# An eight-expert two-layer MLP on one core: TensorE's inner loop cut from eight columns to four, and one critical section in place of two

## The chip, the core and the metric

The kernel runs on one NeuronCore of a Trainium2 chip. Its engines run side by side, each with its own instruction stream: TensorE (PE in the profile; its weight loads are the row PEld), VectorE (DVE), ScalarE (ACT), GpSimd (POOL) and SyncE (SP). A letter q behind a name (PEldq, SPq) means the engine's sequencer, which reads the instructions one after the other, carries out the register, branch and semaphore instructions itself and hands the rest on. Sixteen DMA engines move data between HBM and the core's memory SBUF. TensorE writes its results to a second memory, PSUM, which ScalarE and VectorE read.

The metric is the device time of one execution in microseconds (us), the median of several runs.

## The reference

```python
n_experts, capacity, hidden, expert_hidden = 8, 256, 512, 2048
...
h = np.matmul(x, w1) + b1[:, np.newaxis, :]
h = np.maximum(h, 0)
return (np.matmul(h, w2) + b2[:, np.newaxis, :]).astype(np.float32)
```

For each of eight experts, 256 rows of 512 values are multiplied by a 512 x 2048 matrix, a bias is added and negative values are set to zero; the result is multiplied by a 2048 x 512 matrix and a second bias is added. Inputs and outputs are float32 in HBM. The weights are 8 MB per expert, 64 MB in all.

## The kernel before

**Loading.** GpSimd issues the weight loads (`load_w1`, `load_w2`, both through `load`, line 91), in float32 from HBM to float16 in SBUF. Each of w1 and w2 has three buffers (`NW = 3`); the load into a buffer that was used waits until the matmuls of the expert before have read it. SyncE loads the inputs of experts 0 and 1 at the start, and GpSimd the other inputs in two groups. ScalarE loads the first bias.

**Transposing.** VectorE casts the first two inputs to float16 and transposes each expert's input in 32 x 32 blocks (`transposes`, lines 176 and 179).

**TensorE.** Its program is a loop over eleven steps (line 279). Step s does the first matmul of expert s (if s < 8, line 290) and then the second matmul of expert s - 3 (if s >= 3, lines 311 and 314). The first matmul is cut into 16 columns j of 128 hidden units; a column is four matmuls (kc = 0 to 3) that accumulate into one of four PSUM banks (`j % NPH`). An inner loop (line 286) runs over the columns: before the change it has eight columns in its body and goes round twice per expert. The semaphore `s_credit` counts free banks: the first matmul of column j waits for j + 1, ScalarE adds one when it has read a bank, and at the end of the loop body (line 300) TensorE's sequencer takes off as many as the body has columns. The second matmul is 16 + 16 matmuls of 512 columns into two PSUM banks, each with one matmul for the bias ahead (line 311). TensorE waits for weights and inputs by `take` (line 274). [...]

**Reading PSUM.** ScalarE turns each column of the first matmul into float16 with bias and relu (line 227); it also copies one of the two output banks (line 191), VectorE the other. ScalarE's order is: the sixteen columns of expert s, then the copies of expert s - 3.

**Handing weights over.** SyncE waits for each load's semaphore and adds to `s_go` (`go`, line 240), which `take` consumes. The results of experts 0 to 3 and of 4 and 5 are stored by GpSimd in two large stores (`flush`), those of experts 6 and 7 by SyncE (`store`, line 244), whose last one waits for both output copies (line 264).

**Sections.** All of this stands in one critical section (lines 83 to 325), whose start and end are synchronised by ScalarE: every engine waits for ScalarE's signal before it enters. A second section (line 326) has SyncE wait for the four stores. Then the engines meet at a barrier (line 354).

Of the kernel before, what the change touches and what calls it, by code (L numbers as in the profile page):

```python
# [10 lines left out]
def kernel(  # L11
# [12 lines left out]
    nc = tc.nc  # L24
# [3 lines left out]
    PE = mybir.EngineType.PE  # L28
    E, T, H = x.shape
    M = w1.shape[2]  # L30
    P = 128
    nTB = T // P
    nKC = H // P
    nJ = M // P
    half = nJ // 2
    B = 32
    nB = P // B
    LAG = 3
    NW = 3
    NPH = 4  # L40
    GROUPS = {0: 4, 4: 2}
    HALVED = (E - 2, E - 1)
# [7 lines left out]
    def sem(name):  # L50
        return ctx.enter_context(nc.semaphore(name=name))
# [21 lines left out]
    results = {}  # L73
    for first, n in GROUPS.items():
# [4 lines left out]
    ph = ctx.enter_context(nc.psum_tensor("ph", [P, NPH, H], fp32))  # L79
    po = ctx.enter_context(nc.psum_tensor("po", [P, 2 * nTB * H], fp32))  # L80

    section = ctx.enter_context(ExitStack())
    section.enter_context(tc.tile_critical(  # L83
        sync_engine=mybir.EngineType.Activation, no_gpsimd_drain=True))


    landed = {}

    def load(engine, key, **kw):
        landed[key] = sem(f"d_{key}")  # L90
        engine.dma_start(**kw).then_inc(landed[key], 16)  # L91
# [6 lines left out]
    s_credit = sem("ph_free")  # L98
# [24 lines left out]
    def load_w2(e):  # L123
        if e >= NW:
            nc.gpsimd.wait_ge(s_po[1], e - NW + 1)
        dst = w2_sb[:, e % NW * nJ * H : (e % NW + 1) * nJ * H].rearrange("p (j h) -> p j h", j=nJ)
        src = w2[e].rearrange("(p j) h -> p j h", j=nJ)
        size = half if e in HALVED else nJ
        for lo in range(0, nJ, size):
            load(nc.gpsimd, f"w2_{e}_{lo}", out=dst[:, lo : lo + size], in_=src[:, lo : lo + size])  # L130

    def flush(first):
        n = GROUPS[first]
        for tb in range(nTB):
            nc.gpsimd.wait_ge(s_out[tb], first + n)
        load(nc.gpsimd, f"out{first}", in_=results[first][:],
             out=out[first : first + n].rearrange("e (p r) h -> (e p) r h", r=n * nTB))
# [3 lines left out]
         in_=b2.rearrange("e h -> (e h)").rearrange("(o f) -> o f", o=1))  # L141
    for s in range(1, E + LAG - 1):
# [4 lines left out]
        if s >= LAG:  # L147
            load_w2(s - LAG)
    load_w2(E - 1)
    for first in GROUPS:  # L150
        flush(first)


    nc.vector.memset(ones1[:], 1.0).then_inc(s_ones, 1)  # L154
    nc.scalar.wait_ge(s_ones, 1)
    nc.scalar.activation(out=warm[:], in_=ones1[:], func=relu)  # L156
# [48 lines left out]
    for b in range(nB):  # L205
        last = nc.vector.transpose(  # L206
            out=b1T[b * B : (b + 1) * B, nB - 1 - b : nB - 1 - b + nJ * B],
            in_=b1_rows[:].rearrange("r (i j) -> r j i", j=nJ),
# [9 lines left out]
    for s in range(E + LAG):  # L218
        if s < E:
# [3 lines left out]
            for j in range(nJ):  # L223
# [4 lines left out]
                    out=hT[:, at : at + T].rearrange("p (tb k i) -> p tb k i", tb=nTB, k=split),  # L228
                    in_=ph[:, j % NPH, 0:T].rearrange("p (tb i k) -> p tb k i", tb=nTB, k=split),
# [11 lines left out]

    def store(e, p0, p1, engine):
        dst = out[e].rearrange("(p r) h -> p r h", r=nTB)
        load(engine, f"out{e}_{p0}", out=dst[p0:p1], in_=results[e][p0:p1])

    for s in range(E + LAG):
        if s == 0:
            nc.sync.wait_ge(landed["b2"], 16)
        if s < E:
            go(f"w1_{s}")  # L250
        e = s - LAG
        if e >= 0 and e not in HALVED:
            go(f"w2_{e}_0", 2)
        elif e == E - 2:
            go(f"w2_{e}_0")
            go(f"w2_{e}_{half}")
        elif e == E - 1:
            go(f"w2_{e}_0")
            for tb in range(nTB):
                nc.sync.wait_ge(s_out[tb], e)  # L260
            store(E - 2, 0, P, nc.sync)
            go(f"w2_{e}_{half}")
    for tb in range(nTB):
        nc.sync.wait_ge(s_out[tb], E)
    store(E - 1, 0, P, nc.sync)


    nc.tensor.sem_inc(s_credit, NPH)
# [4 lines left out]
    def take(s, n=1):  # L273
        nc.tensor.wait_ge(s, n).then_inc(s, -n)  # L274

    def at(value, most):
        return nc.tensor.snap(value.with_bounds(min_val=0, max_val=most))

    with nc.Fori(0, E + LAG, 1, engines=[PE], head_slot={PE: 0}) as s:
        nc.tensor.wait_ge(s_credit, NPH)  # L280
        w_at = at(s % NW * (nKC * M), (NW - 1) * nKC * M)
        with nc.tensor.If(s < E):
            x_at = at((s & 1) * (nKC * T), nKC * T)
            take(s_go)
            take(s_xT)
            with nc.Fori(w_at, w_at + nJ, half, engines=[PE]) as w_from:
                w_from = w_from.with_bounds(min_val=0, max_val=(NW - 1) * nKC * M + half)
                for j in range(half):
                    for kc in range(nKC):
                        last = nc.tensor.matmul(  # L290
                            ph[:, j % NPH, 0:T],
                            w1_sb[:, bass.ds(w_from + (kc * M + j), P, nJ)],
                            xT[:, bass.ds(x_at + kc * T, T)],
                            start=(kc == 0),
                            stop=(kc == nKC - 1),
                        )
                        if kc == 0:
                            last.wait_op(s_credit, j + 1, "sem-ge")
                    last.then_inc(s_ph, 1)
                nc.tensor.sem_inc(s_credit, -half)  # L300
        with nc.tensor.If(s >= LAG):
            b_at = at((s - LAG) * H, (E - 1) * H)
            h_at = at(((s + 1) & LAG) * (nJ * T), LAG * nJ * T)
            p_at = at(((s + 1) & 1) * (nTB * H), nTB * H)
            for lo in range(0, nJ, half):
                take(s_go)
                for tb in range(nTB):
                    bank = po[:, bass.ds(p_at + tb * H, H)]
                    if lo == 0:
                        take(s_free[tb])  # L310
                        nc.tensor.matmul(bank, ones1[:], b2_sb[:, bass.ds(b_at, H)],  # L311
                                         start=True, stop=False)
                    for j in range(lo, lo + half):
                        last = nc.tensor.matmul(  # L314
                            bank,
                            hT[:, bass.ds(h_at + (j * T + tb * P), P)],
                            w2_sb[:, bass.ds(w_at + j * H, H)],
                            start=False,
                            stop=(j == nJ - 1),
                        )  # L320
                    if lo:
                        last.then_inc(s_po[tb], 1)


    section.close()
    with tc.tile_critical(sync_engine=mybir.EngineType.SP, no_gpsimd_drain=True):
        for key in (*(f"out{first}" for first in GROUPS), f"out{E - 2}_0", f"out{E - 1}_0"):
            nc.sync.wait_ge(landed[key], 16)


# [28 lines left out]
```

## Time and profile before

| quantity | value |
|---|---|
| median of 3 runs | 183.68 us (182.99 to 183.78) |
| the profiled execution's own time | 183.61 us |
| its span, first to last instruction | 181.8 us |
| mean granted TensorE clock | 0.967 |
| PE busy | 136.5 us (75%) |
| DVE / ACT busy | 87.5 us (48%) / 72.8 us (40%) |
| bytes read from and written to HBM | 71.39 MB and 4.19 MB, 416 GB/s over the span |

The profiled execution's time is 1.8 us more than its span, and 0.07 us under the median of the runs. Times in rows are from the start of the span. In a row of a timeline stand the start, the duration, the engine and line, the operation, its tiles, how many instructions are merged, and in brackets the idle time of that engine before it and what ended it. A row of a list of one line's instructions gives their count, the shortest, median and longest duration in ns, and the first and last start. A row of a table by stretches gives the busy time of each engine, the granted clock, the mean busy share of the 16 DMA engines, and GB/s. In the strips over 40 slices each digit is a busy share in tenths.

### The profile page before, as it was taken

What the parts mean: (1) busy time and instruction counts of PE and PEld (TensorE: products, weight loads), DVE (VectorE), ACT (ScalarE), POOL (GpSimd) and SP (SyncE); (2) the same over time, 40 slices, a digit from 0 to 9 for tenths busy, and PEclk for the clock granted to TensorE, in tenths of its full rate; (3) what the DMA queues carried; (4) which work ended last, traced back from release to release, by engine and by line L of the source; (5) the groups of instructions that cost most, each with busy time, mean ns of one, the idle gap of its engine ahead of it and who ended that gap; (6) DMA issues with size and microseconds to landing.
All of it is one profiled execution on the core that took longest, in us unless ns stands there. A gap on an engine that the chain in (4) does not pass through costs nothing. (4 is left out here: it accounts for less than half of the span.)

```text
span 181.8 us, 3006 instructions
## 1 busy us (share of the span) xinstructions
PE 136.5 (75%) x784; PEld 92.8 (51%) x784; DVE 87.5 (48%) x125; ACT 72.8 (40%) x152; POOL 12.5 (7%) x27
## 2 busy tenths in 40 slices
PE   0000996969969794897988797879799797999940
PEld 0000894859858541694468544874389333444310
DVE  0999936739000199998199708990600030301010
ACT  3000494767747505383077505770397102011010
POOL 6000003020020101001010001000200003010000
PEclk9999997899997999699999999999999999999997
DMA  5989998999999999999999999999999999999991
GB/s 190 282 187 222 231 223 187 223 231 222 196 220 205 241 198 220 227 220 198 220 231 216 198 220 231 220 195 220 231 223 195 216 209 218 213 218 227 419 407 53
DMA packets 3827, 40.48 MB, mean 223 GB/s; under 512 B 448, under 2 KB 464, under 8 KB 1136
## 3 DMA queue, kind: packets, MB, share of 16 engines
q0 software_dynamic: 3200, 38.28, 95.2%
q1 hardware_dynamic: 576, 2.10, 3.1%
q10 hardware_dynamic: 48, 0.07, 0.1%
q8 instruction: 1, 0.02, 0.0%
q14 instruction: 2, 0.02, 0.0%
HBM read 71.39 MB, written 4.19 MB: 416 GB/s over the span
## 5 line engine op out<-in xcount | busy, mean ns | idle before, releaser
L290 PE MATMUL ph<-xT,w_sb 128*128 x512 | 73.6, 309 | 31.9 <-PEq L274 29.8
L290 PEld LDWEIGHTS ph<-xT,w_sb 128*128 x512 | 67.2, 147 | 39.3 <-issue 32.3
L227 ACT ACTIVATE hT<-ph,b1T 128x256 f16<-128x256 f32 x128 | 58.5, 474 | 37.5 <-PE ph L290 34.8
L179 DVE STREAM_TRANSPOSE xT<-x 32x256 f16<-32x256 f16 (+1 forms) x64 | 52.8, 895 | 26.6 <-DMA x<-in_x_dram 21.8
L314 PE MATMUL po<-w_sb,hT 128*128 x256 | 58.2, 380 | 0.3
L314 PEld LDWEIGHTS po<-w_sb,hT 128*128 x256 | 24.2, 98 | 30.5 <-issue 4.8
L191 DVE COPY out<-po 32x512 f32<-32x512 f32 (+1 forms) x20 | 13.7, 687 | 40.9 <-PE po L314 40.6
L191 ACT COPY out<-po 32x512 f32<-32x512 f32 (+1 forms) x20 | 11.6, 578 | 49.9 <-PE po L314 49.8
L91 POOL DMA_DIRECT2D w_sb<-in_w_dram x18 | 9.8, 545 | 139.4 <-PE po L314 72.3
L176 DVE STREAM_TRANSPOSE xT<-x 32x256 f16<-32x256 f16 x32 | 13.9, 436 | 0.5
L311 PE MATMUL po<-b_sb,ones 1*128 x16 | 6.1, 379 | 5.9 <-PEq L274 5.9
L191 DVE COPY x<-po 128x512 f32<-128x512 f32 x2 | 1.4, 692 | 13.7 <-PE po L314 13.7
L311 PEld LDWEIGHTS po<-b_sb,ones 1*128 1x128 f16 x16 | 1.4, 90 | 11.4 <-issue 11.4
L191 ACT COPY x<-po 128x512 f32<-128x512 f32 x2 | 1.2, 585 | 14.0 <-PE po L314 14.0
L206 DVE STREAM_TRANSPOSE b1T<-b_rows 32x512 f32<-32x512 f32 x4 | 4.1, 1022 | 0.1
L200 DVE CAST x<-x 128x1024 f16<-128x1024 f32 x2 | 1.4, 694 | 3.3 <-DMA x<-in_x_dram 3.3
L91 POOL DMA_DIRECT2D out_dram<-out x2 | 1.1, 540 | 9.0 <-ACT out L191 9.0
L156 ACT ACT_TABLE_LOAD x1 | 1.3, 1283 | 1.0 <-ACTq L83 1.0
L91 POOL DMA_DIRECT2D x<-in_x_dram x2 | 1.1, 557 | 0.0
L154 DVE MEMSET ones<- 1x128 f16 x1 | 0.2, 165 | 1.0 <-ACTq L83 1.0
L91 POOL DMA_DIRECT2D b_sb<-in_b_dram x1 | 0.5, 507 | 0.0
L156 ACT ACTIVATE warm<-ones 1x128 f16<-1x128 f16 x1 | 0.3, 308 | 0.0
(4 smaller groups left out, 0.4 us busy)
## 6 DMA issues: line engine op xcount, KB each, us to landing
w_sb<-in_w_dram POOLq DMA_DIRECT2D x14, 2048.0 KB, 40.1
w_sb<-in_w_dram POOLq DMA_DIRECT2D x4, 1024.0 KB, 22.2
out_dram<-out POOLq DMA_DIRECT2D x1, 2048.0 KB, 25.5
x<-in_x_dram SPq DMA_DIRECT2D x2, 512.0 KB, 5.9
x<-in_x_dram POOLq DMA_DIRECT2D x1, 1024.0 KB, 33.9
out_dram<-out POOLq DMA_DIRECT2D x1, 1024.0 KB, 18.7
out_dram<-x SPq DMA_DIRECT2D x2, 512.0 KB, 7.4
x<-in_x_dram POOLq DMA_DIRECT2D x1, 512.0 KB, 25.8
```

The lines of the kernel that those rows point to most:

```text
L91: engine.dma_start(**kw).then_inc(landed[key], 16)
L154: nc.vector.memset(ones1[:], 1.0).then_inc(s_ones, 1)
L156: nc.scalar.activation(out=warm[:], in_=ones1[:], func=relu)
L176: last = nc.vector.transpose(out=dst[:, :, g, :, 0, :], in_=block[:, :, :, 0, :])
L179: last = nc.vector.transpose(out=dst[:, tb, g], in_=block[:, tb])
L191: last = copy(out=results[e][at : at + rows, k * nTB + tb, :], in_=po[k * rows : (k + 1) * rows, bank : bank + H])
L200: nc.vector.tensor_copy(out=x16[e][0][:], in_=x32[e][:]).then_inc(s_self, 1)
L206: last = nc.vector.transpose(out=b1T[b * B : (b + 1) * B, nB - 1 - b : nB - 1 - b + nJ * B], in_=b1_rows[:].rearrange("r (i j) -> r j i", ...
L227: nc.scalar.activation(out=hT[:, at : at + T].rearrange("p (tb k i) -> p tb k i", tb=nTB, k=split), in_=ph[:, j % NPH, 0:T].rearrange("p ( ...
L290: last = nc.tensor.matmul(ph[:, j % NPH, 0:T], w1_sb[:, bass.ds(w_from + (kc * M + j), P, nJ)], xT[:, bass.ds(x_at + kc * T, T)], start=(k ...
L311: nc.tensor.matmul(bank, ones1[:], b2_sb[:, bass.ds(b_at, H)], start=True, stop=False)
L314: last = nc.tensor.matmul(bank, hT[:, bass.ds(h_at + (j * T + tb * P), P)], w2_sb[:, bass.ds(w_at + j * H, H)], start=False, stop=(j == nJ ...
```

## The change

There are three parts.

1. The inner loop of the first matmul has four columns (`NPH`) in its body and goes round four times per expert. Bank `j % NPH` becomes bank `j`; the sequencer takes off four credits at the end of each body. TensorE's instruction listing has 121 rows after the change, 155 before. [...]
2. One section instead of two. It is synchronised by SyncE. The two large stores are awaited by SyncE inside the section, at its end; the last two stores count on a semaphore of their own, `s_last`, which is awaited behind the section. VectorE adds 32 to it ahead of the section and takes 32 off inside it.
3. A call ahead of GpSimd's two stores (`wait_critical_data_deps`) takes GpSimd's wait for the section's start out of the entry and puts it there: GpSimd enters without waiting, and issues the weight loads at once.

```diff
+    s_last = sem("last_stores")
+    nc.vector.sem_inc(s_last, 16 * len(HALVED))
...
-        sync_engine=mybir.EngineType.Activation, no_gpsimd_drain=True))
+        sync_engine=mybir.EngineType.SP, no_gpsimd_drain=True))
...
     load_w2(E - 1)
+    tc.wait_critical_data_deps()
     for first in GROUPS:
         flush(first)
...
+    nc.vector.sem_inc(s_last, -16 * len(HALVED))
     nc.vector.memset(ones1[:], 1.0).then_inc(s_ones, 1)
...
-        load(engine, f"out{e}_{p0}", out=dst[p0:p1], in_=results[e][p0:p1])
+        engine.dma_start(out=dst[p0:p1], in_=results[e][p0:p1]).then_inc(s_last, 16)
...
     store(E - 1, 0, P, nc.sync)
+    for first in GROUPS:
+        nc.sync.wait_ge(landed[f"out{first}"], 16)
...
-    with nc.Fori(0, E + LAG, 1, engines=[PE], head_slot={PE: 0}) as s:
+    with nc.Fori(0, E + LAG, 1, engines=[PE]) as s:
...
-            with nc.Fori(w_at, w_at + nJ, half, engines=[PE]) as w_from:
-                w_from = w_from.with_bounds(min_val=0, max_val=(NW - 1) * nKC * M + half)
-                for j in range(half):
+            with nc.Fori(w_at, w_at + nJ, NPH, engines=[PE]) as w_from:
+                w_from = w_from.with_bounds(min_val=0, max_val=(NW - 1) * nKC * M + nJ - NPH)
+                for j in range(NPH):
...
-                            ph[:, j % NPH, 0:T],
+                            ph[:, j, 0:T],
...
-                nc.tensor.sem_inc(s_credit, -half)
+                nc.tensor.sem_inc(s_credit, -NPH)
...
     section.close()
-    with tc.tile_critical(sync_engine=mybir.EngineType.SP, no_gpsimd_drain=True):
-        for key in (*(f"out{first}" for first in GROUPS), f"out{E - 2}_0", f"out{E - 1}_0"):
-            nc.sync.wait_ge(landed[key], 16)
+    nc.sync.wait_ge(s_last, 16 * len(HALVED))
```

## The prediction

> **What bounds the kernel now.** I read the strips of the page first, then the waits of TensorE and SyncE, then TensorE's timeline.
>
> ```profile
> DMA  5989998999999999999999999999999999999991
> q8 instruction: 1, 0.02, 0.0%
> ...
> PE ph L290 <- PEq L274: 29.8, 8, 17.9
> ...
> SPq L240 <- DMA w_sb<-in_w_dram: 150.2, 17, 14.6
> ```
>
> The DMA engines are busy from end to end, and SyncE spends 150.2 us waiting for weights. But how far is TensorE behind them? The next fence puts TensorE's starts beside the moments at which SyncE hands over w1 of experts 4, 5 and 6 (line 240).
>
> ```profile
> 17.87 9.82 PE L290 MATMUL ph<-xT,w_sb 128*128 x64 [17.87 <-PEq L274]
> 29.47 9.68 PE L290 MATMUL ph<-xT,w_sb 128*128 x64 [1.78 <-PEq L274]
> 40.93 4.38 PE L290 MATMUL ph<-xT,w_sb 128*128 x32 [1.78 <-PEq L274]
> 52.02 9.30 PE L290 MATMUL ph<-xT,w_sb 128*128 x64 [1.77 <-PEq L274]
> 62.30 0.37 PE L311 MATMUL po<-b_sb,ones 1*128 x1 [0.98 <-PEq L274]
> 64.83 5.35 PE L314 MATMUL po<-w_sb,hT 128*128 x24
> 73.54 9.57 PE L290 MATMUL ph<-xT,w_sb 128*128 x64 [3.35 <-PEq L274]
> ...
> L240 SPq EVENT_SEMAPHORE  x1: 17/17/17, 72.6 to 72.6; - x1
> L240 SPq EVENT_SEMAPHORE  x1: 17/17/17, 92.0 to 92.0; - x1
> L240 SPq EVENT_SEMAPHORE  x1: 17/17/17, 111.4 to 111.4; - x1
> ...
> 105.71 5.35 PE L314 MATMUL po<-w_sb,hT 128*128 x24
> 112.24 4.38 PE L290 MATMUL ph<-xT,w_sb 128*128 x32 [1.18 <-PEq L274]
> 117.15 4.39 PE L290 MATMUL ph<-xT,w_sb 128*128 x32 [0.53 <-ACT hT L227]
> 122.51 0.37 PE L311 MATMUL po<-b_sb,ones 1*128 x1 [0.96 <-PEq L274]
> ...
> w_sb<-in_w_dram POOLq DMA_DIRECT2D x14, 2048.0 KB, 40.1
> ```
>
> Weights come every 19.4 us (72.6, 92.0, 111.4). TensorE ends a step at 105.71 + 5.35 = 111.06, only 0.3 us before the weights of the next. Once, ahead of expert 4, it has slack: done at 64.83 + 5.35 = 70.18, weights at 72.6, 2.4 us. So DMA and TensorE are nearly level: what makes a step of TensorE longer by more than about 0.3 us makes TensorE the bound. The weight loads are issued 40.1 us ahead of their landing, four loads deep, so a TensorE that is some us late in freeing a buffer does not let the DMA engines run dry.
>
> **Part 1, the inner loop.** What does one closing of the loop cost? TensorE's sequencer, near 116 us:
>
> ```profile
> L300 PEldq EVENT_SEMAPHORE  x1: 51/51/51, 116.3 to 116.3; - x1
> L286 PEldq FUSED_REGOPS  x1: 42/42/42, 116.5 to 116.5; - x1
> L286 PEldq COMPARE_BRANCH  x1: 215/215/215, 116.6 to 116.6; - x1
> L290 PEldq FUSED_REGOPS  x4: 46/60/79, 116.1 to 117.2; - x4
> ...
> 117.14 0.60 PEld L290 LDWEIGHTS ph<-xT,w_sb 128*128 x4 [0.72 <-ACT hT L227]
> ...
> 111.10 2.34 ACT L191 COPY out<-po 32x512 f32<-32x512 f32 x4 [8.38 <-PE po L314]
> 113.63 3.50 ACT L227 ACTIVATE hT<-ph,b1T 128x256 f16<-128x256 f32 x8 [0.19 <-PE ph L290]
> 117.98 0.47 ACT L227 ACTIVATE hT<-ph,b1T 128x256 f16<-128x256 f32 x1 [0.85 <-PE ph L290]
> ```
>
> The profile puts the 0.72 us of idle weight loads at 117.14 down to ScalarE. But ScalarE had read all eight columns by 113.63 + 3.50 = 117.13 and then waited itself for TensorE; the ninth column needs only the bank of the fifth. The idle time is filled by the sequencer: 0.7 us from the semaphore at 116.3 past the branch to the first register operation. Inside the body the loads follow without a gap. After the branch the first four register operations take up to 79 ns in place of 46, about 0.1 us more. I take 0.84 us a closing. Per expert the loop closes after columns 4, 8 and 12 in place of 8: two more, 1.7 us of sequencer time. The bounds: nothing, if the wait really is ScalarE's (ScalarE reads a column in 0.47 us whatever the loop); 0.9 us a closing, if it also starts slower.
>
> Steps 0 to 3 wait for no weights but the first. Their starts lie 11.60, 11.46, 11.09 and 10.28 us apart (17.87, 29.47, 40.93, 52.02, 62.30). The third ran at full clock and shows the sequencer's pace; with 1.7 us more it takes 12.8, and the first two, slowed by the clock at their start, come to the same pace. The fourth takes 12.0. Sum 50.4 in place of 44.4: 6.0 us more, beyond the 2.4 us of slack. From expert 4 on TensorE waits for nothing.
>
> A step of TensorE that waits for nothing: from the end of the second matmul (111.06) ScalarE copies until 113.44 and frees the first bank at 113.63 + 0.47 = 114.1, 3.0 us after; the fifth column needs it, and the closing after column 4 is hidden there. From 114.1 to the next bias matmul (122.51) are 8.4 us with one closing, 9.2 with two. From the bias matmul to the end of the second matmul are 70.18 - 62.30 = 7.9. Sum 3.0 + 9.2 + 7.9 = 20.1, against 19.4 between weights. Four such steps, 80.4 us.
>
> At the end, experts 5 to 7, and the close:
>
> ```profile
> 150.91 0.37 PE L311 MATMUL po<-b_sb,ones 1*128 x1 [1.17 <-PEq L274]
> 168.95 5.64 PE L314 MATMUL po<-w_sb,hT 128*128 x24
> L91 SPq DMA_DIRECT2D out_dram<-x x1: 344/344/344, 175.3 to 175.3; - x1
> DMA to landing us min/median/max: 5.1/5.1/5.1
> ...
> 178.00:179.00 1.00, 0.00 (x0) 0.00 (x0) 0.00 (x0) 0.00 (x0) 0.00 (x0) 1.00 0.06 25
> 179.00:180.00 1.00, 0.00 (x0) 0.00 (x0) 0.00 (x0) 0.00 (x0) 0.00 (x0) 1.00 0.06 25
> ...
> L354 SPq EVENT_SEMAPHORE  x5: 28/28/4345, 176.1 to 181.0; - x5
> ```
>
> They take 168.95 + 5.64 - 150.91 = 23.7 us, and the last store is issued 0.7 us after (175.3 against 174.59). It lands in 5.1 us, of which the last 2.0 (178 to 180) have a DMA share of 0.06, one engine of sixteen: one engine is late, and everything that counts sixteen landings is as late. With idle DMA engines I take 3.0 us for the landing (bounds 2.6 and 5.1).
>
> **Part 1, the instruction block.** What makes one engine late? In the window 4 to 7 us the DMA view has an instruction transfer:
>
> ```profile
> q8 instruction: 1, 0.02, 2.0%
> ```
>
> 2.0% of 16 engines over 3 us is 0.96 us on one engine, on the way of the first weights. It is the only transfer of its queue, 16 KB. If it is TensorE's next block, a program within one block does without, and the first weights land about 1.0 us earlier (bounds 0 and the 2.0 us of the end). No row names the engine it serves; two chances in three that it goes.
>
> [...]
>
> **Parts 2 and 3.** GpSimd's first load starts at 1.48, after a wait for ScalarE until 1.04. Its own barrier ends at 0.6.
>
> ```profile
> 1.48 0.67 POOL L91 DMA_DIRECT2D w_sb<-in_w_dram  x1 [1.04 <-ACTq L83]
> L343 POOLq EVENT_SEMAPHORE  x2: 17/17/17, 0.5 to 0.6; - x2
> ```
>
> So its loads can move up by at most 0.4 us (1.04 - 0.6); SyncE's loads of the inputs go to the same DMA engines at that time, so I take 0.1 (bounds 0 and 0.4). GpSimd's wait for the section's start, now ahead of its two large stores, has long been met there. SyncE gives the section's signal itself, and the other engines enter when they did. VectorE's two semaphore instructions cost nothing beside its wait for the input. Behind the last landing SyncE has, from 180.4 (176.1 + 4.3) on, three more waits, a branch and the second section's signals until 181.2; now one signal and the barrier remain. I take 0.5 us off (bounds 0.7, and 0.3 more should GpSimd, which now leaves the section later, be late at the barrier). The waits for the two large stores end earlier than the last store does; behind them on SyncE stands only the close.
>
> **The sum.** First matmul 17.87 - 1.0 - 0.1 = 16.8; + 50.4 + 7.9 + 80.4 + 23.7 = 179.2, end of TensorE's work; + 0.7 to the store, + 3.0 landing = 182.9; + 0.9 (181.8 - 180.4 - 0.5) = 183.8, the span; + 1.8 outside it: 185.6, against 183.61 for the execution read and 183.68 for the median.
>
> **Rivals.**
>
> 1. *The closings are hidden* (the wait was ScalarE's, or the sequencer runs ahead), and the block's transfer is gone. Then DMA stays the bound, all sixteen engines end together: 183.61 - 2.0 - 0.5 = 181.1. For it speaks the releaser that the profile names; against it ScalarE's 0.85 us of waiting at 117.98. It decides if a closing costs under about 0.3 us. [...] The branch's row has 215 ns, and it is one of several instructions.
> 2. *The block's transfer stays*, the closings cost: 186.6.
> 3. *The block's transfer stays and the closings are hidden*: the change does only its part 2: 183.0.
> 4. *The clock.* TensorE's first matmul gets thinner, and the clock is halved for a stretch after a thin one:
>
> ```profile
> 50.29:53.70 3.41, 1.68 (x13) 1.66 (x13) 0.00 (x0) 1.26 (x3) 1.06 (x2) 1.00 0.90 192
> 53.70:57.12 3.42, 3.42 (x19) 2.70 (x18) 0.00 (x0) 2.04 (x5) 0.00 (x0) 0.50 0.99 208
> 60.53:63.94 3.41, 2.41 (x14) 1.36 (x13) 1.01 (x1) 1.23 (x3) 0.53 (x1) 1.00 1.13 240
> ```
>
> Busy 1.68 of 3.41 us was followed by half clock, 2.41 was not. A stretch with one end of the first matmul and a closing or two comes between. Half clock over 3.4 us of the second matmul costs 1.7: 187.3 with one such stretch, more with two.
>
> **How the numbers follow.** The forecast case 0.44 (its own range 184.4 to 186.8: 0.1 us on a closing's price is 0.2 us in each of the steps 0 to 3 and 0.1 in each of the next four, 1.2 in all); rival 1 0.18, rival 2 0.18, rival 3 0.08, rival 4 0.12. The range goes from rival 1 to rival 4: 181.0 to 188.2. About 0.5% (0.9 us) is what a measurement can tell from no change. Slower by more: the forecast case almost whole, rivals 2 and 4, 0.68; faster: rival 1, 0.19; the rest 0.13.
>
> **What would show it.** Right: starts of line 290 (299 in the changed file) 12.8 us apart; idle weight loads of 0.7 us after every fourth column; no q8 row; no TensorE wait for weights after expert 3; bias matmuls 20.1 us apart from expert 0 to 4; DMA share falling well before the last store. Wrong: bias matmuls still 19.4 us apart with waits at `take`, or a q8 row as before.

## The result and the profile after

The changed kernel takes 184.23 us (median; 184.13 to 184.60), the kernel before 183.26 us beside it: a ratio of 1.0055 (95% interval 1.0040 to 1.0071), 1.0 us slower. The forecast was 185.6, on the right side and inside its range, but 1.4 us high. The kernel before came out lower as well, 183.26 in place of the 183.68 that the prediction had. So the forecast loss was 1.9 us and the measured one 1.0.

The profiled execution has a span of 182.7 us and a time of 184.60. Its strips of DMA and clock, and the last rows of its DMA queues:

```profile
DMA  5989998999999998999999999999899989999972
...
PEclk9999998898899999999999999999999999999999
...
q10 hardware_dynamic: 48, 0.07, 0.1%
q14 instruction: 2, 0.02, 0.0%
```

The q8 row, which stood between these two in the kernel before, is gone, and the DMA strip falls to 7 and 2 before the end, where it stood at 9 to the last slice but one. TensorE's timeline (start, duration, engine and line, operation, tiles, count, idle time before and what ended it):

```profile
16.62 5.31 PE L299 MATMUL ph<-xT,w_sb 128*128 x32 [16.62 <-PEq L283]
29.46 5.56 PE L299 MATMUL ph<-xT,w_sb 128*128 x32 [1.74 <-PEq L283]
42.28 8.11 PE L299 MATMUL ph<-xT,w_sb 128*128 x48 [1.78 <-PEq L283]
55.04 2.35 PE L299 MATMUL ph<-xT,w_sb 128*128 x16 [1.74 <-PEq L283]
...
67.06 0.37 PE L320 MATMUL po<-b_sb,ones 1*128 x1 [0.98 <-PEq L283]
...
94.87 1.91 PE L299 MATMUL ph<-xT,w_sb 128*128 x16
98.13 2.32 PE L299 MATMUL ph<-xT,w_sb 128*128 x16 [1.35 <-ACT hT L234]
100.99 2.35 PE L299 MATMUL ph<-xT,w_sb 128*128 x16 [0.54 <-ACT hT L234]
...
147.34 0.37 PE L320 MATMUL po<-b_sb,ones 1*128 x1 [0.95 <-PEq L283]
155.17 0.38 PE L320 MATMUL po<-b_sb,ones 1*128 x1
173.15 5.35 PE L323 MATMUL po<-w_sb,hT 128*128 x24
```

The steps 0 to 3 start 12.8 us apart (16.62, 29.46, 42.28, 55.04), and the first bias matmul comes at 67.06. From there the bias matmuls stand (147.34 - 67.06) / 4 = 20.07 us apart. Expert 5's first matmul starts at 94.87 with no idle time before it: TensorE no longer waits for weights, and it is the bound. The first closing of such a step hides behind ScalarE (1.35 us at 98.13); the others show as 0.54 us of idle PE. The second matmuls of experts 5 to 7 follow without a gap, and TensorE ends at 173.15 + 5.35 = 178.50.

The end, by stretches of 1 us (busy times, granted clock, mean DMA share, GB/s), and in lists of one line's instructions the store, SyncE's last wait (1750 ns, from 180.1) and GpSimd's last drain:

```profile
177.00:178.00 1.00, 1.00 (x6) 0.48 (x5) 0.50 (x1) 0.00 (x0) 0.00 (x0) 1.00 0.15 61
178.00:179.00 1.00, 0.50 (x3) 0.01 (x1) 0.00 (x0) 0.46 (x1) 0.00 (x0) 1.00 0.00 0
...
L251 SPq DMA_DIRECT2D out_dram<-x x2: 344/346/347, 171.5 to 179.2; - x2
DMA to landing us min/median/max: 2.6/4.7/6.7
...
L88 SPq EVENT_SEMAPHORE  x4: 17/22/1750, 179.8 to 180.1; - x4
...
L360 POOLq DRAIN  x3: 45/78/1929, 179.9 to 182.4; - x3
```

The DMA engines have run dry when the last store is issued at 179.2. It lands in 2.6 us, at 180.1 + 1.75 = 181.85, and the span ends 0.8 us after.

### The profile page after: what moved, and what is told of

Same layout as the page of the kernel before. It is cut to its first block, busy times and chain, and to the rows that moved or that the text cites. A ratio compares the mean times of both kernels' runs of the same rounds, so it can differ in the third digit from the quotient of the medians.

```text
span 182.7 us, 3079 instructions
## 1 busy us (share of the span) xinstructions
PE 137.7 (75%) x784; PEld 92.5 (51%) x784; DVE 87.5 (48%) x125; ACT 72.8 (40%) x152; POOL 12.5 (7%) x27
## 5 line engine op out<-in xcount | busy, mean ns | idle before, releaser
L299 PE MATMUL ph<-xT,w_sb 128*128 x512 | 75.7, 305 | 35.8 <-PEq L283 21.9
L320 PEld LDWEIGHTS po<-b_sb,ones 1*128 1x128 f16 x16 | 1.4, 90 | 10.3 <-issue 10.3
## 6 DMA issues: line engine op xcount, KB each, us to landing
out_dram<-out POOLq DMA_DIRECT2D x1, 1024.0 KB, 13.1
```

The costliest lines, as they stand in the source:

```text
L299: last = nc.tensor.matmul(ph[:, j, 0:T], w1_sb[:, bass.ds(w_from + (kc * M + j), P, nJ)], xT[:, bass.ds(x_at + kc * T, T)], start=(kc == 0 ...
```

## The experiments

All times are medians beside runs of the kernel before on the same chip. Theory A is the prediction's: a closing of the inner loop costs TensorE's sequencer 0.84 us, which makes TensorE the bound, and the 16 KB transfer is what made one DMA engine late.

**Part 1 alone.** The kernel before with this edit only, four columns in a body and no slot (`head_slot`) for the outer loop:

```diff
-    with nc.Fori(0, E + LAG, 1, engines=[PE], head_slot={PE: 0}) as s:
+    with nc.Fori(0, E + LAG, 1, engines=[PE]) as s:
...
-            with nc.Fori(w_at, w_at + nJ, half, engines=[PE]) as w_from:
+            with nc.Fori(w_at, w_at + nJ, NPH, engines=[PE]) as w_from:
...
-                nc.tensor.sem_inc(s_credit, -half)
+                nc.tensor.sem_inc(s_credit, -NPH)
```

> The kernel before with part 1 alone: four columns a loop body, no slot for the outer loop; two sections and GpSimd's awaited entry as before. Theory A (a closing costs TensorE's sequencer 0.84 us and makes TensorE the bound; the 16 KB block transfer delays one DMA engine, and it goes with the shorter program): no q8 row, starts of the first matmul 12.8 us apart, bias matmuls 20.1 us apart, the close as long as before: about 0.6 us above the changed kernel's 184.2, so 184.8. Theory B (the idle time after four columns is ScalarE's bank credit, closings are free; the changed kernel is slow for another reason, in its sections): starts 11.5 apart as before and about 181.3. Theory C (the gain at the start comes from GpSimd's unawaited entry and not from the block): the last landing of each weight load is 1.0 us late as before, the first matmul starts at 17.7, about 185.8.

Measured: 184.85 us, ratio 1.0080 (1.0065 to 1.0095). TensorE's first two steps:

```profile
16.77 5.37 PE L290 MATMUL ph<-xT,w_sb 128*128 x32 [16.77 <-PEq L274]
...
29.61 5.58 PE L290 MATMUL ph<-xT,w_sb 128*128 x32 [1.74 <-PEq L274]
```

There is no q8 row; the first matmul is at 16.77, the steps are 12.8 us apart, the bias matmuls 20.07. GpSimd's first load starts at 1.5 as before, and SyncE hands over the first weights 1.1 us earlier all the same (15.9 against 17.0): the earlier first matmul comes with the missing transfer and not from GpSimd's entry. Theories B and C fall. Against the whole change, 0.15 us of the 0.6 are at the start (16.77 against 16.62), the rest at the close: from the landing (182.0) to the end it takes 1.4 us, in the changed kernel 0.8.

**Eight columns again, without the slot.** The changed kernel with the old loop body:

```diff
-            with nc.Fori(w_at, w_at + nJ, NPH, engines=[PE]) as w_from:
+            with nc.Fori(w_at, w_at + nJ, half, engines=[PE]) as w_from:
...
-                nc.tensor.sem_inc(s_credit, -NPH)
+                nc.tensor.sem_inc(s_credit, -half)
```

> The changed kernel with eight columns in the loop body again, all else as changed (no slot, one section, GpSimd unawaited). Theory A: TensorE has its old pace, DMA is the bound. If the longer program still goes without the q8 transfer: 16.6 for the first matmul, all sixteen engines end together, 180.8 to 181.1. If the q8 transfer is back: 182.7. Theory B: nothing is gained from the loop, 184.2 as the changed kernel. Theory C: 181.0 with or without a q8 row.

Measured: 183.07 us, ratio 0.9992 (0.9975 to 1.0009). DMA queues in the window 28 to 32 us, TensorE's first steps, and the last stretches:

```profile
q8 instruction: 1, 0.02, 1.5%
...
16.50 9.74 PE L299 MATMUL ph<-xT,w_sb 128*128 x64 [16.50 <-PEq L283]
28.22 4.45 PE L299 MATMUL ph<-xT,w_sb 128*128 x32 [1.99 <-PEq L283]
39.46 9.45 PE L299 MATMUL ph<-xT,w_sb 128*128 x64 [1.79 <-PEq L283]
...
178.00:179.00 1.00, 0.00 (x0) 0.00 (x0) 0.00 (x0) 0.00 (x0) 0.00 (x0) 0.50 0.11 45
179.00:180.00 1.00, 0.00 (x0) 0.00 (x0) 0.00 (x0) 0.00 (x0) 0.00 (x0) 0.50 0.04 16
```

The transfer comes in the window 28 to 32 us, about where the second step starts, against 4.9 in the kernel before. That the longer program runs into its next block there by itself is the author's estimate; no row shows a block. The first weights are early (16.50), TensorE does not stop (28.22 to 39.46 is 11.2 us, 29.47 to 40.93 in the kernel before is 11.5), and at the end one or two of sixteen engines work alone (shares of 0.11 and 0.04 from 178 to 180). So the lateness follows the transfer and not the section. The time is 0.4 us over the 182.7 expected for this case; the next experiment shows where that is.

**Parts 2 and 3 alone.** As the last one, with the slot:

```diff
-    with nc.Fori(0, E + LAG, 1, engines=[PE]) as s:
+    with nc.Fori(0, E + LAG, 1, engines=[PE], head_slot={PE: 0}) as s:
...
-            with nc.Fori(w_at, w_at + nJ, NPH, engines=[PE]) as w_from:
+            with nc.Fori(w_at, w_at + nJ, half, engines=[PE]) as w_from:
```

> Parts 2 and 3 alone: the changed kernel with eight columns in the loop body and with the outer loop placed at a slot, as before. Theory A: the q8 row is there, last landings 1.0 us late, first matmul at 17.7 (0.1 to 0.2 earlier than 17.87), the close 0.5 us shorter: 182.6 to 182.8 against 183.3 before. Theory B: the sections are what slows the changed kernel: about 184. Theory C: first matmul at 16.7, no late landing in spite of a q8 row, about 181.1.

Measured: 183.41 us, ratio 1.0007 (0.9992 to 1.0021): no gain, where every theory but B saw one, and B's 184 is not reached either. The first matmul starts at 17.57, 0.3 us earlier. The close is not shorter. SyncE's last wait and GpSimd's drains:

```profile
L88 SPq EVENT_SEMAPHORE  x4: 17/22/750, 178.6 to 178.9; - x4
...
L360 POOLq DRAIN  x3: 45/78/1929, 178.7 to 181.0; - x3
L360 POOLq EVENT_SEMAPHORE  x4: 17/17/17, 180.7 to 181.2; - x4
```

The last store has landed at 178.9 + 0.75 = 179.65. GpSimd's drain starts at 178.7, when the section ends, takes 1.93 us, and only then, at 180.7, GpSimd enters the barrier, 1.0 us after the landing. The same line in the kernel before:

```profile
L354 POOLq DRAIN  x3: 45/84/5547, 174.8 to 181.6; - x3
```

There the section ended ahead of the waits for the stores, and the drain was over (174.8 + 5.5 = 180.3) when the last store landed at 180.4. It took 5.5 us, not 1.93, and GpSimd's own second store was under way when it began:

```profile
L91 POOL DMA_DIRECT2D out_dram<-out x2: 536/540/543, 151.1 to 160.6; - x2
...
out_dram<-out POOLq DMA_DIRECT2D x1, 1024.0 KB, 18.7
```

That store landed at 160.6 + 18.7 = 179.3, and the drain ended 1.0 us after. So the drain is not a fixed 1.93 us: with GpSimd's stores home it takes that long from its start, and with one of them still out it lasted beyond the landing. Moving the two waits into the section puts the drain behind the landing of the large stores. Where TensorE is the bound this is free: the second of those stores is home at 164.8 + 13.1 = 177.9, and the drain (179.94 + 1.93 = 181.87) ends with the last landing (181.85).

**The slot put back.** The changed kernel, with four columns:

```diff
-    with nc.Fori(0, E + LAG, 1, engines=[PE]) as s:
+    with nc.Fori(0, E + LAG, 1, engines=[PE], head_slot={PE: 0}) as s:
```

> The changed kernel with the outer loop placed at a slot again, and nothing else. Theory A (the 16 KB transfer costs the first weights about 1 us and, where TensorE is the bound, nothing more, since the DMA engines fall idle ahead of the last store): the q8 row is back near 4.8 us, the first matmul starts at 17.6 to 17.9 in place of 16.6, the steps stay 12.8 and 20.07, and the time is 185.2 to 185.4. Rival (the transfer is a passenger, and the earlier first matmul comes from GpSimd's earlier entry): first matmul at 16.6 and 184.2. Second rival (the late engine costs at the end too, as it did before the change): 186.3 or more.

Measured: 185.19 us, ratio 1.0103 (1.0084 to 1.0122). The queue in the window 4 to 7 us, TensorE's first start, the stretches ahead of the last store, and the store's:

```profile
q8 instruction: 1, 0.02, 2.4%
...
17.64 8.29 PE L299 MATMUL ph<-xT,w_sb 128*128 x48 [17.64 <-PEq L283]
...
178.00:179.00 1.00, 1.00 (x6) 0.39 (x4) 0.26 (x1) 0.00 (x0) 0.00 (x0) 1.00 0.30 123
179.00:180.00 1.00, 0.26 (x2) 0.00 (x0) 0.00 (x0) 0.59 (x1) 0.00 (x0) 1.00 0.07 29
...
181.00:182.00 1.00, 0.00 (x0) 0.00 (x0) 0.00 (x0) 0.00 (x0) 0.00 (x0) 1.00 0.99 406
```

The one argument brings the transfer back, the first matmul starts 1.02 us later (17.64 against 16.62), and the time is 0.96 us more (0.7 against the second measurement of the changed kernel, below). The DMA share is down to 0.07 from 179 to 180, and the last store then moves at a share of 0.99 from 181 to 182: here, where the engines fall idle ahead of it, the late one has caught up, and the transfer costs its 1.0 us once.

**A longer closing.**

```diff
                 nc.tensor.sem_inc(s_credit, -NPH)
+                for _ in range(4):
+                    nc.tensor.sem_inc(s_dummy, 1)
+                    nc.tensor.sem_inc(s_dummy, -1)
```

> The changed kernel with eight more semaphore instructions (four pairs of plus one and minus one on a semaphore that nobody awaits) in each closing of the inner loop. Theory A: the sequencer is what TensorE waits for, so each of the four closings per expert grows by the same d (eight times 0.06 to 0.15 us: 0.5 to 1.2 us); steps 0 to 3 grow by 4d each, and the period from expert 4 on by 3d, since the closing after column 4 hides behind ScalarE's copies as long as it takes under 1.35 us plus its own time; 28d in all, 198 to 218 us. Theory B (the idle time after four columns is ScalarE's bank credit, 0.7 us): up to 0.7 us more per closing change nothing, 184 to 190.

Measured: 218.58 us, in a single run, just above the range expected. TensorE's timeline:

```profile
16.54 3.63 PE L300 MATMUL ph<-xT,w_sb 128*128 x16 [16.54 <-PEq L284]
...
51.97 3.63 PE L300 MATMUL ph<-xT,w_sb 128*128 x16 [2.20 <-PEq L284]
56.07 2.82 PE L300 MATMUL ph<-xT,w_sb 128*128 x16 [0.47 <-issue]
60.16 2.35 PE L300 MATMUL ph<-xT,w_sb 128*128 x16 [1.27 <-ACT hT L235]
...
86.51 0.37 PE L324 MATMUL po<-b_sb,ones 1*128 x1 [2.19 <-PEq L284]
...
181.33 0.37 PE L324 MATMUL po<-b_sb,ones 1*128 x1 [0.88 <-PEq L284]
```

The first four steps take 86.51 - 16.54 = 69.97 us in place of 50.44: 19.53 over 16 closings, 1.22 each. The period from expert 4 on is (181.33 - 86.51) / 4 = 23.7 in place of 20.07: 3.6, or 1.2 for each of the three closings that do not hide. The granted clock is lower here (0.878 on average), but that is not what lengthens the steps: the groups of four columns start 4.1 us apart (51.97, 56.07, 60.16) whether one takes 3.63 us or 2.35. What the sequencer gets more to do, TensorE loses whole. ScalarE's credit would have taken up the first 0.7 us.

**No closing.** All sixteen columns written out:

```diff
-            with nc.Fori(w_at, w_at + nJ, NPH, engines=[PE]) as w_from:
...
-                for j in range(NPH):
+            for j in range(nJ):
```

> The changed kernel with all sixteen columns written out and no inner loop; TensorE's program is longer than one block. Theory A: starts of the first matmul in steps 0 to 3 at full clock 11.09 - 0.84 = 10.25 us apart in place of 12.8; DMA is the bound; at least one q8 transfer, so one engine late: as the kernel before, 182.7 to 183.3. Theory B: starts 11.1 apart as with eight columns, or 11.6.

Measured: 183.41 us, ratio 0.9997 (0.9977 to 1.0017), one q8 transfer in the window 28 to 32 us. TensorE:

```profile
16.56 9.12 PE L297 MATMUL ph<-xT,w_sb 128*128 x64 [16.56 <-PEq L283]
27.07 8.69 PE L297 MATMUL ph<-xT,w_sb 128*128 x64 [1.40 <-PEq L283]
...
49.91 8.52 PE L297 MATMUL ph<-xT,w_sb 128*128 x64 [1.39 <-PEq L283]
59.15 0.37 PE L318 MATMUL po<-b_sb,ones 1*128 x1 [0.71 <-PEq L283]
```

Step 0 takes 10.5 us and step 3, up to the bias matmul, 9.2. So:

| columns in a body | a step, start to start | step 3, to the bias matmul |
|---|---|---|
| 16 | 10.5 | 9.2 |
| 8 (before) | 11.1 | 10.3 |
| 4 (changed) | 12.8 | 12.0 |
| 4, closing longer by 1.2 | 17.7 | 16.9 |

The two closings from eight to four cost 1.7 us, 0.86 each. Taking away the loop altogether, which leaves one semaphore instruction behind the sixteen columns, saves another 0.6 us in the one place and 1.0 in the other, where 0.84 was expected; why these differ was not pursued. The time does not follow: the DMA strip stands at 9 up to the last slice but one, as in the kernel before, with one q8 transfer as there.

**The second matmul in a loop.** To have eight columns and a short program, the second matmul is rolled instead:

```diff
+            with nc.Fori(0, 2 * 7, 7, engines=[PE]) as lo:
+                take(s_go)
...
+                for tb in range(nTB):
+                    for j in range(7):
+                        second(tb, j, h_lo, w_lo, False)
+            for tb in range(nTB):
+                for j in range(2 * 7, nJ):
+                    last = second(tb, j, h_at, w_at, j == nJ - 1)
```

> The changed kernel with eight columns in the first matmul's loop body, and the second matmul put into a loop of two rounds of seven columns with the last two columns behind it, so that TensorE's program stays short; the order of the second matmul's products changes, the sums are the same. Theory A with the closing of the second matmul's loop hidden behind its matmuls (0.23 us each, paced by TensorE itself): no q8 row, DMA the bound, 181.0. Theory A with that closing not hidden: 0.84 us more per expert, a step of TensorE 19.9 us: about 183. Theory B: no better than the changed kernel, 184.2.

Measured: 183.14 us, ratio 0.9987 (0.9960 to 1.0014), in two groups: 182.2 to 182.6 and 183.7 to 184.4. No q8 row within the span. The profiled execution is of the upper group. Its timeline and two stretches (the last three columns are granted clock, DMA share, GB/s):

```profile
82.70 0.66 PE L325 MATMUL po<-b_sb,ones 1*128 x2 [0.79 <-PEq L283]
83.87 7.08 PE L315 MATMUL po<-w_sb,hT 128*128 x32 [0.51 <-issue]
...
103.16 8.76 PE L315 MATMUL po<-w_sb,hT 128*128 x32 [0.48 <-issue]
...
101.43:104.84 3.41, 2.34 (x8) 0.93 (x9) 2.23 (x2) 0.28 (x1) 0.00 (x0) 0.88 1.01 216
104.84:108.25 3.41, 3.41 (x11) 1.33 (x10) 0.00 (x0) 0.00 (x0) 0.00 (x0) 0.61 0.97 207
```

The loop's entry adds 0.5 us of idle PE right behind the gap at the bias matmul, and in three of the experts the clock is halved in the stretch after it: the second matmul takes 8.76 in place of 7.08 us, 1.7 more. That is the prediction's rival 4, with its price, in another kernel. The 183 us of the second expectation came out, but not by its cause: no closing of the second matmul's loop shows within the 32 matmuls.

**The same with cover.** One column ahead of the loop, one behind it:

```diff
+            for tb in range(nTB):
+                second(tb, 0, h_at, w_at, False)
             with nc.Fori(0, 2 * 7, 7, engines=[PE]) as lo:
...
-                    for j in range(7):
+                    for j in range(1, 8):
...
+                second(tb, nJ - 1, h_at, w_at, True).then_inc(s_po[tb], 1)
```

> Like the kernel with the second matmul in a loop of two rounds, but with its first column ahead of the loop and its last one behind it, so that two matmuls run while the sequencer sets up the loop. Expected: no q8 transfer within the span, TensorE's gap at the bias matmuls 0.4 us shorter than in that kernel; if that is enough to keep the clock from being halved, every run at 182.2, the lower of the two groups in which that kernel's runs lie (182.2 to 182.6 and 183.7 to 184.4); if not, 183.1 again.

Measured: 182.40 us (181.93 to 183.81), ratio 0.9964 (0.9941 to 0.9986): faster than the kernel before by 0.7 us by the ratio (183.32 to 182.40, 0.9, by the medians), the one version here that beats both kernels clear of the noise. The idle time at the loop's entry falls from 0.5 to 0.2 us. Not every run is at 182.2, as was expected if the cover kept the clock from being halved: half are under it, the others reach to 183.8; the profile is of one of the lowest (181.97), so what slows the others was not seen. The last stretches and GpSimd's drain:

```profile
177.00:178.00 1.00, 0.00 (x0) 0.00 (x0) 0.00 (x0) 0.00 (x0) 0.00 (x0) 1.00 0.82 332
178.00:179.00 1.00, 0.00 (x0) 0.00 (x0) 0.00 (x0) 0.00 (x0) 0.00 (x0) 1.00 0.00 0
...
L368 POOLq DRAIN  x3: 45/78/1929, 177.6 to 179.9; - x3
```

TensorE ends as in the kernel before (167.78 + 6.65 = 174.4), the store is issued at 175.1, and all engines end together at 178, where the kernel before had one working on to 180. Of these 2.0 us the drain gives back a part: it ends at 177.6 + 1.93 = 179.5, 1.0 us after the landing.

**The large stores awaited outside again.** The last kernel with the two waits in a second section:

```diff
-    for first in GROUPS:
-        nc.sync.wait_ge(landed[f"out{first}"], 16)
...
     section.close()
+    with tc.tile_critical(sync_engine=mybir.EngineType.SP, no_gpsimd_drain=True):
+        for first in GROUPS:
+            nc.sync.wait_ge(landed[f"out{first}"], 16)
```

> The kernel with the second matmul in a loop (first column ahead of it, last one behind) and with the waits for the two large stores moved out of the section into a second one, as in the kernel before. Theory (GpSimd's last drain takes at least 1.93 us from the end of the section, and where DMA is the bound it is what the closing barrier waits for): the section ends at about 175.2 in place of 177.5, the drain is over before the last store has landed, and the end comes about 1.4 us after that landing in place of 1.7; 182.1. Rival (the drain waits for the stores themselves): the drain ends as late as before, no gain or 0.3 us more, 182.4 to 182.7.

Measured: 182.55 us, ratio 0.9975 (0.9948 to 1.0002). In the trace the drain starts at 176.9, is over at 178.8, ahead of the landing at 179.0, and the end comes 1.5 us after that landing in place of 1.7. The 0.2 to 0.3 us does not show in the time, whose runs spread over 2 us: 182.55 lies in the range of the rival. That the earlier section gives an earlier drain is seen, its worth in time is not. Nor does this run test the rival's cause, since GpSimd's last store was home (161.7 + 15.6 = 177.3) soon after the drain began; the 5.5 us of the kernel before speak for it. The clock was halved in this profile too, though only 0.2 us of idle PE were left at the loop's entry:

```profile
103.54 8.33 PE L313 MATMUL po<-w_sb,hT 128*128 x30 [0.20 <-issue]
...
124.61 6.65 PE L313 MATMUL po<-w_sb,hT 128*128 x30 [0.24 <-issue]
```

Three of the eight second matmuls took 8.33 us in place of 6.65. So the cover did not do away with the halved clock, and the 0.5 us of the kernel without it is not shown to be what brings it on.

**The changed kernel again**, unedited:

> The changed kernel once more, for a second trace of it. If its time is set by TensorE's fixed pace, 184.2 with little spread, steps of 12.8 and 20.07 us again; what differs from the first trace lies at the start (first weights) and in the landing of the last store.

Measured: 184.49 us (184.26 to 184.94), ratio 1.0068 (1.0046 to 1.0091). First matmul at 16.46, first bias matmul at 66.89, the next ones 20.08 us apart, a span of 182.5. The pace repeats to a few hundredths of a us; the loss is 1.0 to 1.3 us. Differences to the changed kernel that were taken from its first measurement, 184.23, are 0.3 us smaller against this one.

## Why the prediction was right in direction and wrong in size

- **What bounds, and the turn to TensorE: right.** Slack of 0.3 us in a step, 0.7 us more per step (20.1 against 19.4), TensorE bound from expert 0 on: 20.07 measured.
- **The price of a closing, 0.84 us: right.** 0.86 from eight to four columns, and the sum of the first four steps (50.4) came out at 50.44. The reading that the profile's releaser (ScalarE) was not the cause is shown by part 1 alone, by the longer closing and by the missing one, so rival 1 falls. The row of a branch that goes round has 217 ns in the changed kernel (at 60.3), a quarter of a closing.
- **The 16 KB transfer: right, and sharper than forecast.** 1.0 us at the start forecast, 1.02 measured by putting the slot back. Rival 2 (the transfer stays) is that kernel: 0.7 to 0.96 us above the changed one, where the prediction had 1.0 (186.6 against 185.6). TensorE's step did not grow where the transfer comes between 28 and 32 us (11.2 us with eight columns and no slot), while the landings at the end were late there (shares of 0.11 and 0.04 from 178 to 180). That the transfer is TensorE's next block, and that a short enough program does without, was the author's estimate, and no row shows whose instructions it carries. The runs show when it comes: with the slot, or with eight or sixteen columns and no slot; not with four columns and no slot, nor with eight and the second matmul in a loop.
- **Parts 2 and 3: right in the changed kernel, wrong by themselves.** First weights 0.15 us earlier (0.1 forecast), the close 0.6 us shorter (0.5 forecast). But with DMA as the bound the step "0.3 more should GpSimd, which now leaves the section later, be late at the barrier" is what happens, and more than that: the whole gain is gone. Rival 3 (183.0) describes that kernel, which came out at 183.41, with a close 0.3 us longer (1.7 against 1.4 from landing to end) in place of 0.5 shorter.
- **The steps that failed are the last terms of the sum.** "They take 168.95 + 5.64 - 150.91 = 23.7 us" took over a stretch of the kernel before in which the last second matmul still waited for weights: 5.64 for its last 24 matmuls, 5.35 after, and in the kernel before SyncE hands over the last weights at 170.6 and TensorE's `take` follows at 170.7. TensorE that waits for nothing does the three in 178.50 - 155.17 = 23.3. That is 0.4 us. The landing, taken as 3.0 with bounds from 2.6, is 2.6, with a DMA share of 0.00 in the 1 us before the store is issued: another 0.4. The 3.0 was an estimate near the 5.1 - 2.0 = 3.1 that the last store of the kernel before took without the stretch of one engine alone; the 2.6 of the bound was the author's own, since the shortest landing in that kernel (line 91) is 3.5. The first matmul is 0.2 us earlier than summed and the four steps together 0.1 shorter. Together 1.1 us of span (183.8 forecast, 182.7 measured); the time outside it is 1.9 in place of 1.8.
- **The reference.** The profiled execution (184.60) is the slowest of its runs, 0.4 us over their median; the sum was made for one execution and given as the median. The kernel before came out 0.4 lower than its first three runs. The first widens the miss of the absolute time (1.0 to 1.4), the second takes as much off the miss of the loss (1.4 to 0.95). That the two nearly cancel is chance.
- **Rival 4** does not decide: in the changed kernel the clock is at 1.00 from 47.3 us to the end. A halved second matmul is seen where it is rolled, at the 1.7 us that the rival had for it. But what the prediction shows, 1.68 us busy of 3.41 halved and 2.41 not, leaves the border open: in the kernel without cover, 3.41 us with 2.11 busy (from 80.97) were followed by a clock of 1.00, and with 2.12 busy (from 121.89) by 0.61.

## What to carry to other kernels

When two resources are level, price both sides of a change: here 1.7 us of sequencer time per expert turned a kernel bound by DMA into one bound by TensorE, and of the 2 us for which one DMA engine worked alone at the end, at most 1.0 came back. When the bound changes, rebuild every later term under the new bound; a stretch copied from the old trace carries the old waits with it. Look at a loop's closing where the sequencer is the bottleneck, and put it behind matmuls long enough to cover it: here it showed behind matmuls of 0.15 us (16 in 2.35 us), and not in the loop of the second matmul, whose matmuls take 0.22 us (32 in 7.08 us).

## What the runs showed of the hardware

- One 16 KB instruction transfer (1.5% of sixteen engines over 4 us, 2.4% over 3 us: 0.96 to 1.15 us on one engine) makes what spreads over the sixteen engines land about as much later for as long as they have no idle time: SyncE hands over the first weights at 17.0 in the kernel before and w1 of expert 4 at 72.6, and at 15.9 and 71.5 in part 1 alone, which has no transfer. At the end of the kernel before one engine works alone for up to 2.0 us (178 to 180, share 0.06), more than the transfer took; why more is open. With the slot put back in the changed kernel, where the share falls to 0.07 from 179 to 180, the last store had 0.99 again. The transfer came at 4.9 us in the kernel before, between 4 and 7 with the slot put back, and between 28 and 32 for eight and sixteen columns without it.
- GpSimd's drain at the end takes 1.93 us from the end of the section in the changed kernel and in four of the experiments (eight columns without the slot, parts 2 and 3 alone, the second matmul in a loop with cover, two sections again). In parts 2 and 3 alone, where the last store landed within that time, GpSimd came to the barrier 1.0 us after the landing (180.7 against 179.65). In the kernel before, where a store of GpSimd's own was still out when the drain began, it took 5.5 us.
- Semaphore instructions cost TensorE's sequencer 0.15 us each (1.22 us for eight), though the row of such an instruction shows 51 ns; what follows one in the changed kernel's own closing starts 0.15 us after it as well (60.00 and 60.15).
- With 0.5 us more of idle PE behind the bias matmul, the clock was halved for 3.4 us in three of eight second matmuls, 1.7 us each. With 0.2 us there it was halved in one second matmul of one profile (8.33 in place of 6.65 us) and in three of another. What decides is open.
